# Gate tanh tiles in a ring of their own, alternating parities in the Toeplitz products, later copies of the powers, and two merge gates loaded early, in a hybrid S5 and dilated-attention layer

## The chip, the cores and the metric

The kernel runs on one core of a Trainium2 chip. The metric is the device time of one execution in microseconds (us). A core has a matmul engine (PE, with a separate weight-load row PEld in the profile), a vector engine (DVE), a scalar engine (ACT), a general engine (POOL), and a queue engine (SP) that here only issues transfers. All run their own instruction streams in order and wait for each other through semaphores. Matmul results land in PSUM, which has eight banks; everything else lives in SBUF, in 128 partitions.

## The reference, cut to what matters

One decoder layer of 512 tokens with 1024 channels, in float32. One projection feeds two branches and two merge gates:

```python
h = rms_norm(x, norm_w)
u_s, z_s, q, k, v, z_a, r_s, r_a = split(h @ w_in)
y_s = s5_branch(u_s, ...)                  # diagonal complex scan, GELU, GLU with w_glu
y_s = (y_s * silu(z_s)) @ w_ssm_out
y_a = dilated_attention(norm_rope(q), norm_rope(k), v)   # 3 dilations, 8 heads of 64
y_a = (y_a * silu(z_a)) @ w_attn_out
m = sigmoid(r_s) * y_s + sigmoid(r_a) * y_a
out = x + m @ w_o
```

The sigmoid is computed as a tanh of half the argument: sigmoid(r) = (tanh(r/2) + 1)/2, and silu likewise; the halves are folded into later scales.

## The kernel before, in words

**Matmuls.** A float32 product is made from three fp32r matmuls (`mm3`, L108 to L110): each operand is split into a high part (ACT, L93) and a remainder (DVE, L95), and high x high, high x low and low x high are added up in PSUM. A projection unit (`cm_unit`) takes 128 output channels for all 512 tokens: 8 blocks of the contraction by 3, so 24 matmuls of 128x512 into one bank named `pj`. In the first half of the program there are three such banks and five general ones (tag `g`); in the second half four, three and one for attention outputs. Weights arrive by SP (`w_raw`, two buffers of 512 KB), are split by ACT and DVE into `w_hi` and `w_lo` (three buffers each), and are fetched two units ahead.

**Stages.** (1) Norm of x and its transposes; the input u of the S5 branch, eight units. (2) Powers of the 64-state transition: they are computed on DVE with groups along partitions (`pw`), turned by small matmuls against an identity into `atp` (32 matmuls in one bank: i is the real or imaginary part, k the power) and `ftp` (4 matmuls, a factor for B), and copied by ACT into `AT` (L405) and `fT` (L411). `AT` feeds all coefficient products (`coef`, L261 to L263) and the scan; `fT` feeds `BB`. (3) The S5 branch in chunks of 8 time steps: `w_unit` and `x_unit` make the chunk inputs, DVE scans over chunks (`scan_work`), and for each of eight blocks j: `ca_unit` makes coefficients, `m_unit` the Toeplitz block (products `kps`, 16 matmuls of 64x16 weights against 128 columns on tiles of the array given by `tile_position`; ACT copies to `kt`, POOL adds the skip term and sends eight transfers into M), `y_unit` the outputs (`yps`) and `g_unit` the transposes (`yT`) and the GELU (`gs`, `gq`). Between them stand "fillers": gate units of the same projection, in the order za (4), zs (8), two for v, rs (8), ra (2). (4) GLU with w_glu, then w_ssm_out with the gate r_s, giving `m1`. (5) Attention for four pairs of heads, with projections of q, k and v between scores and values; the remaining six ra units lie here, one ahead of the pairs and five behind the last scores. (6) w_attn_out in eight blocks c: the gate is loaded (`ral`, L1103), DVE forms (ral + 1) x projection + m1 (L1108, L1109), which is split for the last product with w_o; the residual x is loaded whole (`xr`, 2 MB) and added.

**Gates.** Every gate unit ends in one tanh on ACT from its `pj` bank into a tile `th`. For za and zs (`silu2`) DVE multiplies at once. For rs and ra the tile is stored in DRAM (`gd[1, c]`, `rad[c]`) by SP and loaded again when it is used.

**Buffers and order.** The helper `t2k` hands out tiles of 128x512 from a ring of six buffers with one tag. `th`, `ysb`, `gs`, `gq`, `z`, `ral` and others share it. A tile's buffer becomes free when the last reader is through, a transfer included. The framework orders the instructions: each engine gets a fixed list, drawn up when the program is built from a simulated timeline, the order of the text serving as priority. So the lists can differ from the text, and an edit in one place can change them elsewhere. It also sets all waits; instructions that touch one PSUM bank wait for each other.

Of the kernel before, what the change touches and what calls it, by code (L numbers as in the profile page):

```python
# [11 lines left out]
F32 = mybir.dt.float32  # L12
# [8 lines left out]
P = 128  # L21
# [6 lines left out]
Q = 16  # L28
# [24 lines left out]
def tile_hybrid_block(ctx: ExitStack, tc: tile.TileContext, x, positions, norm_w, w_in, lam_re, lam_im,  # L53
# [3 lines left out]
    pe, act, dve, pool, sp = nc.tensor, nc.scalar, nc.vector, nc.gpsimd, nc.sync  # L57
# [5 lines left out]
    tmp = ctx.enter_context(tc.tile_pool(name="tmp", bufs=6))  # L63
# [21 lines left out]
    def bank(name):  # L85
        return ps_g.tile([P, 512], F32, name=name, tag="g")

    def t2k(name, dtype=F32):
        return tmp.tile([P, 512], dtype, name=name, tag="t2k")
# [23 lines left out]
    n_ra = 2  # L113
# [66 lines left out]
    def cm_unit(rh, rl, kts=KT):  # L180
        hi, lo = get_w()
        ps = ps_p.tile([P, 512], F32, name="pj", tag="pj")
        for k in range(kts):
            mm3(ps, hi[:, k], lo[:, k], rh[:, k], rl[:, k], k == 0, k == kts - 1)
        return ps
# [28 lines left out]
    for h in range(2):  # L214
# [10 lines left out]
        for q in range(KT // 2):  # L225
            ps = bank("hps")
# [133 lines left out]
    pw = big.tile([G, 2, 9, N], F32, name="pw", tag="s7a")  # L360
# [20 lines left out]
    for n in (1, 2, 4):  # L381
# [3 lines left out]
        a = pw[:, :, 0:n, :]  # L385
# [6 lines left out]
    H = G // 2  # L392
    AT = cst.tile([P, 2, H, 9], F32, name="AT")
    fT = cst.tile([P, 2, H], F32, name="fT")
    pool.memset(AT[:, 0, :, 8:9], 1.0)
    pool.memset(AT[:, 1, :, 8:9], 0.0)
    idg = ident[:G, :G].rearrange("p (m two) -> p two m", two=2)
    ps = bank("atp")
    for i in range(2):
        for k in range(8):  # L400
            for h in range(2):
                o = i * 8 * H + (7 - k) * H
                pe.matmul(ps[64 * h:64 * h + 64, o:o + H], pw[:, i, k], idg[:, h], start=True, stop=True,
                          skip_group_check=True)
        act.copy(AT[:, i, :, 0:8], ps[:, i * 8 * H:(i + 1) * 8 * H].rearrange("p (k g) -> p g k", k=8))  # L405
    ps = bank("ftp")
    for i in range(2):
        for h in range(2):
            pe.matmul(ps[64 * h:64 * h + 64, i * H:(i + 1) * H], pw[:, i, 8], idg[:, h], start=True, stop=True,
                      skip_group_check=True)  # L410
    act.copy(fT.rearrange("p a g -> p (a g)"), ps[:, 0:2 * H])  # L411

    A4 = cst.tile([P, 2, 2, H], F32, name="A4")
    for i in range(2):
# [7 lines left out]
    BB = dd[:, 2560:4096].rearrange("p (a g q) -> p a g q", a=3, g=H)  # L422
# [29 lines left out]
    sza = cst.tile([P, NP, S], F32, name="sza")  # L452
    gd = dram.tile([2, KT, P, S], F32, name="gd")

    def silu2(dst, ps):

        th = t2k("th")
        act.activation(th, ps, AF.Tanh, scale=0.5)
        dve.scalar_tensor_tensor(dst, th, 1.0, ps, op0=ALU.add, op1=ALU.mult)

    def za_unit(c):
        ps = cm_unit(hT_hi, hT_lo)
        silu2(sza[:, c], ps)
# [6 lines left out]

    def rs_unit(c):
        ps = cm_unit(hT_hi, hT_lo)
        th = t2k("th")
        act.activation(th, ps, AF.Tanh, scale=0.5)  # L474
        sp.dma_start(gd[1, c], th)

    rad = dram.tile([KT, P, S], F32, name="rad")

    def ra_unit(c):
        ps = cm_unit(hT_hi, hT_lo)  # L480
        th = t2k("th")
        act.activation(th, ps, AF.Tanh, scale=0.5)  # L482
        sp.dma_start(rad[c], th)

# [43 lines left out]
    for g in range(NG):  # L528
        for a in range(2):
# [3 lines left out]
                      start=True, stop=True, skip_group_check=True)  # L533
# [31 lines left out]
    def v0_unit(hp, V):  # L565
        ps = cm_unit(hT_hi, hT_lo)
        vt = t2k("vt")
        act.copy(vt.rearrange("p (b r j) -> p r b j", r=4, b=4), ps.rearrange("p (r b j) -> p r b j", r=4, b=4))

        def finish():  # L570
            pt = bank("vtp")
            for b in range(NB):
                pe.transpose(pt[:, b * P:(b + 1) * P], vt[:, b * P:(b + 1) * P], ident)
            act.copy(V[:, 0].rearrange("p b c -> p (b c)"), pt)
        return finish
# [17 lines left out]
    H = G // 2  # L593
# [105 lines left out]
    def m_unit(j, ca, dg):  # L699

        kt = big.tile([Q, 8, T, Q], F32, name="kt", tag=("s7a", "s7b")[j % 2])
        ps = bank("kps")
        for gg in range(8):
            a, b, h, m = gg % 4, gg // 4, gg % 2, gg // 2
            for c in range(2):
                sl = slice(64 * h, 64 * h + 64)
                pe.matmul(ps[32 * a:32 * a + Q, b * P:(b + 1) * P], BB[sl, 1 + c, 4 * j + m, :], ca[sl, c, m, 1:9, :],  # L707
                          start=c == 0, stop=c == 1, skip_group_check=True, tile_position=(64 * h, 32 * a))
        kv = kt.rearrange("q (b a) k p -> q a b (k p)", a=4)
        for a in range(4):  # L710
            act.copy(kv[:, a], ps[32 * a:32 * a + Q, 0:2 * P].rearrange("q (b m) -> q b m", b=2))  # L711
        pool.tensor_tensor(kt[:, :, T - 1, :], kt[:, :, T - 1, :], dg, op=ALU.add)  # L712

        M = Mb[j % 3]
        for t in range(T):
            pool.dma_start(M[Q * t:Q * t + Q, :, 0:P - Q * t], kt[:, :, t:].rearrange("q g k p -> q g (k p)"))  # L716
        return M
# [118 lines left out]
    def qk_turn(g, raw, QT, KA, KB):  # L836
        for a in range(2):
            ps = bank("qtp")
            pn = ps.rearrange("p (b r j) -> p r b j", r=4, b=4)
            for r in range(NB):  # L840
                o = pn[:, r] if g == 0 else ps[:, r * P:(r + 1) * P]
                pe.transpose(o, raw[:, r, a * P:(a + 1) * P], ident)  # L842
            if a == 0 or g == 0:
                parts = [(slice(0, P), QT[0][:, g], QT[1][:, g]) if a == 0 else (slice(0, P), KA[0], KA[1])]
            else:
                parts = [(slice(64 * h, 64 * h + 64), KB[0][64 * h:64 * h + 64, g - 1, h],
                          KB[1][64 * h:64 * h + 64, g - 1, h]) for h in range(2)]
            for sl, hi, lo in parts:
                w = wcol[sl, g, a:a + 1]
                act.activation(hi, ps[sl], AF.Copy, scale=w)  # L850
                dve.scalar_tensor_tensor(lo, ps[sl], w, hi.bitcast(F32), op0=ALU.mult, op1=ALU.subtract)  # L851
# [9 lines left out]
    def qk_first(mid=None):  # L861

        pss = wide_granule(hT_hi, hT_lo, mid)
        raws = [new_raw(0), new_raw(1)]
        sq = sml.tile([P, NB, 8], F32, name="ssq")
        for r in range(NB):
            for i in range(2):
                act.copy(raws[i][:, r], pss[r][:, 256 * i:256 * i + 256])
            squares(sq[:, r], pss[r])
        qk_norm((0, 1), raws, sq)  # L870
        return raws

    def qk_second(hp, mid=None):

        pss = wide_granule(hT_hi, hT_lo, mid)
        raw = new_raw(0)
        V = new_v()
        sq = sml.tile([P, NB, 8], F32, name="ssq")[:, :, 0:4]
        for r in range(NB):
            act.copy(raw[:, r], pss[r][:, 0:256])  # L880
            squares(sq[:, r], pss[r][:, 0:256])
            act.copy(V[:, 1:3, r], pss[r][:, 256:512].rearrange("p (g c) -> p g c", g=2))
        qk_norm((2,), [raw], sq)
        return raw, V
# [138 lines left out]
    for c in range(KT):  # L1023
# [5 lines left out]
        ps = cm_unit(gT_hi, gT_lo)  # L1029
        th = t2k("gth")  # L1030
# [4 lines left out]
    for c in range(KT):  # L1035
        r = t2k("rl")
        sp.dma_start(r, gd[1, c])
        ps = cm_unit(yT_hi, yT_lo)
# [28 lines left out]
    ra_unit(n_ra)  # L1067
    qk_turn(2, raw, *QK)

    for hp in range(NP):  # L1070
        Pt = scores(hp, *QK)
        if hp < NP - 1:
            raws = qk_first()

            def mid(kq):
                if kq in (1, 2):
                    qk_turn(kq - 1, raws[kq - 1], *QK)
                if kq == 3:
                    values(hp, Pt, V)

            raw, V_next = qk_second(hp + 1, mid)
            V = V_next
            finv = v0_unit(hp + 1, V)
            qk_turn(2, raw, *QK)
            finv()
        else:
            for c in range(n_ra + 1, KT - 2):
                ra_unit(c)
            values(hp, Pt, V)
            for c in range(KT - 2, KT):  # L1090
                ra_unit(c)
# [6 lines left out]
    for cc in range(KT // 2):  # L1098
        hi, lo = get_w()
        for c2 in range(2):  # L1100
            c = 2 * cc + c2
            th = t2k("ral")
            sp.dma_start(th, rad[c])  # L1103
            ps = ps_p.tile([P, 512], F32, name="pj", tag="pj")
            for k in range(NP):
                mm3(ps, hi[:, k, c2 * P:(c2 + 1) * P], lo[:, k, c2 * P:(c2 + 1) * P], aT[:, 0, k], aT[:, 1, k],
                    k == 0, k == NP - 1)
            dve.scalar_tensor_tensor(th, th, 1.0, ps, op0=ALU.add, op1=ALU.mult)  # L1108
            dve.tensor_tensor(th, th, m1[:, c], op=ALU.add)  # L1109
            split(mT_hi[:, c], mT_lo[:, c], th, scale=0.5)  # L1110
# [38 lines left out]
```

## Time and profile before

| | us |
|---|---|
| median of 3 runs | 743.11 (741.96 to 743.18) |
| profiled execution, its time | 742.37 |
| profiled execution, its span | 740.6 |
| PE busy | 699.8 (94%) |
| DVE busy | 454.2 (61%) |
| ACT busy | 314.8 (43%) |
| POOL busy | 193.9 (26%) |
| mean granted clock of PE | 0.987 |

In the profile's rows, "idle 5.6 <-ACT th L474" or "[1.59 <-ACT th L474]" is idle time of an engine and the instruction that ended it. Timeline rows give the start, the duration, the engine, the line of the kernel, the operation and the tiles as out<-in; "x4" means that several instructions are merged into one row. SPq rows are the issue of transfers, not their landing. A float32 matmul outside `mm3` is recorded as two instructions, so 16 matmuls of a Toeplitz unit are 32 in the profile. In windows, "(x8)" behind an engine's busy time is the number of its instructions, and the three last figures are the granted clock of PE, the share of the transfer engines and GB/s.

### The profile page before, as it was taken

Reading aid. Unit: us, or ns where it says so; the run is one execution under the profiler, and the core shown is the slowest. Engines: PE = TensorE matmul, PEld = TensorE weight load, DVE = VectorE, ACT = ScalarE, POOL = GpSimd, SP = SyncE. Lnnn points to the kernel's source line nnn. Section 1 sums busy time; section 2 is a strip of 40 time slices with the busy share of each in tenths; the row PEclk is TensorE's granted clock in tenths of the full one; section 3 lists DMA queues with packets and bytes.
Section 4 is the critical chain, followed back from the end, with each engine's and each line's share of the span. In section 5 each row is a group of like instructions: output and inputs, shape, how many; then the busy total and the mean of one; then the engine's idle time right before and its main releaser. Section 6 shows DMA issues by size and latency. Waiting matters only on the chain.

```text
span 740.6 us, 12691 instructions
## 1 busy us (share of the span) xinstructions
PE 699.8 (94%) x4821; PEld 572.7 (77%) x4821; DVE 454.2 (61%) x912; ACT 314.8 (43%) x631; POOL 193.9 (26%) x346
## 2 busy tenths in 40 slices
PE   2789999999999898999999999999999989998997
PEld 2778878789877686888889888787778767887886
DVE  6859746989755743673426669647663765464742
ACT  6434543423244564431244465437344643543310
POOL 3426720421122522540002316012412232120000
PEclk9999999999999999999999999999999999999999
DMA  8334654554454644555332322222302230327441
GB/s 203 102 100 129 170 115 104 141 144 120 117 118 106 119 117 129 171 171 170 86 96 80 101 82 85 58 85 58 96 20 86 58 115 12 106 97 240 131 142 57
DMA packets 137213, 82.14 MB, mean 111 GB/s; under 512 B 32696, under 2 KB 125632, under 8 KB 137024
## 3 DMA queue, kind: packets, MB, share of 16 engines
q1 hardware_dynamic: 135088, 78.96, 37.5%
q0 software_dynamic: 2048, 2.36, 2.3%
q8 instruction: 38, 0.62, 0.4%
q14 instruction: 23, 0.19, 0.1%
q10 hardware_dynamic: 16, 0.00, 0.0%
HBM read 68.46 MB, written 10.49 MB: 107 GB/s over the span
## 4 chain that ended last, share of the span: by engine, by line
PE 88%; ACT 4%; DMA 3%; SPq 2%; DVE 2%; issue 0%; ACTq 0%; DVEq 0%
PE pj L108 24%; PE pj L110 24%; PE pj L109 24%; PE ptp L999 2%; DMA w_raw<-in_w_in_dram 2%; PE ot L985 2%; PE kps L707 1%; DMA ral<-rad 1%; PE yps L731 1%; PE yps L738 1%; PE xps L293 1%; PE wps L282 1%; PE sps L929 1%; ACT w_hi L93 1%; PE qtp L842 1%; SPq L426 1%
## 5 line engine op out<-in xcount | busy, mean ns | idle before, releaser
L93 ACT ACTIVATE w_hi<-w_raw 128x1024 fp32r<-128x1024 f32 x100 | 106.0, 1061 | 233.2 <-PE pj L109 133.7
L95 DVE TENSOR_TENSOR w_lo<-w_raw,w_hi 128x1024 fp32r<-128x1024 f32 x98 | 123.7, 1262 | 120.1 <-ACT w_hi L93 119.5
L108 PE MATMUL pj<-hT_hi,w_hi 128*128 128x512 f32 (+1 forms) x344 | 133.1, 390 | 7.8 <-ACT th L474 5.6
L109 PE MATMUL pj<-hT_lo,w_hi 128*128 128x512 f32 (+1 forms) x344 | 132.5, 386 | 4.1 <-DVE hT_lo L236 4.1
L110 PE MATMUL pj<-hT_hi,w_lo 128*128 128x512 f32 (+1 forms) x344 | 132.4, 386 | 0.8 <-DVE w_lo L95 0.8
L109 PE MATMUL pj<-w_lo,hT_hi 128*128 128x512 f32 (+1 forms) x288 | 106.5, 370 | 0.0
L108 PE MATMUL pj<-w_hi,hT_hi 128*128 128x512 f32 (+1 forms) x288 | 106.5, 371 | 0.0
L110 PE MATMUL pj<-w_hi,hT_lo 128*128 128x512 f32 (+1 forms) x288 | 106.0, 371 | 0.0
L108 PEld LDWEIGHTS pj<-hT_hi,w_hi 128*128 128x128 f32 x344 | 65.0, 190 | 22.8 <-ACT th L474 6.8
L109 PEld LDWEIGHTS pj<-hT_lo,w_hi 128*128 128x128 f32 x344 | 65.4, 190 | 17.5 <-DVE hT_lo L236 4.9
L110 PEld LDWEIGHTS pj<-hT_hi,w_lo 128*128 128x128 f32 x344 | 65.5, 190 | 14.4 <-DVE w_lo L95 1.0
L108 PEld LDWEIGHTS pj<-w_hi,hT_hi 128*128 128x128 f32 x288 | 54.0, 188 | 10.1 <-issue 0.2
L110 PEld LDWEIGHTS pj<-w_hi,hT_lo 128*128 128x128 f32 x288 | 54.0, 188 | 10.0
L109 PEld LDWEIGHTS pj<-w_lo,hT_hi 128*128 128x128 f32 x288 | 54.0, 188 | 9.8
L908 ACT ACTIVATE Pt<-Pt,st 128x256 f32<-128x256 f32 (+1 forms) x64 | 31.0, 491 | 18.7 <-DVE st L906 18.7
L829 POOL TENSOR_TENSOR rt<-qraw,tC 128x256 f32<-128x256 f32 x12 | 14.3, 1190 | 87.7 <-DVE qraw L823 87.4
L712 POOL TENSOR_TENSOR kt<-kt,dg 16x128 f32<-16x128 f32 x8 | 5.6, 702 | 116.8 <-ACT kt L711 116.8
L716 POOL DMA_DIRECT2D dd<-kt x64 | 33.8, 537 | 2.4 <-POOL kt L712 2.4
L938 POOL COPY sw<-st 32x4 f32<-32x4 f32 x64 | 12.0, 188 | 73.1 <-ACT Pt L908 70.4
L851 DVE SCALAR_TENSOR_TENSOR qkp<-qtp,wcol,qkp 128x512 fp32r<-128x512 f32 (+1 forms) x32 | 23.0, 745 | 13.2 <-ACT qkp L850 13.1
L850 ACT ACTIVATE qkp<-qtp,wcol 128x512 fp32r<-128x512 f32 (+1 forms) x32 | 20.8, 686 | 15.7 <-PE qtp L842 10.4
L108 PE MATMUL pj<-gT_hi,w_hi 128*128 128x512 f32 x64 | 24.9, 391 | 2.6 <-ACT th L482 2.6
(267 smaller groups left out, 1306.5 us busy)
## 6 DMA issues: line engine op xcount, KB each, us to landing
w_raw<-in_w_in_dram SPq DMA_DIRECT2D x40, 512.0 KB
w_raw<-in_w_in_dram SPq DMA_DIRECT2D x112, 128.0 KB
w_raw<-in_w_glu_dram SPq DMA_DIRECT2D x8, 512.0 KB
w_raw<-in_w_ssm_out_dram SPq DMA_DIRECT2D x8, 512.0 KB
w_raw<-in_w_o_dram SPq DMA_DIRECT2D x8, 512.0 KB
x_all<-in_x_dram SPq DMA_DIRECT2D x4, 512.0 KB
ud<-uT SPq DMA_DIRECT2D x8, 256.0 KB
Uj<-ud SPq DMA_DIRECT2D x8, 256.0 KB
```

The source lines that it names most:

```text
L93: act.activation(hi, src, AF.Copy, scale=scale)
L95: e.tensor_tensor(lo, src, hi.bitcast(F32), op=ALU.subtract)
L108: pe.matmul(o, lh, rh, start=first, stop=False, skip_group_check=True)
L109: pe.matmul(o, lh, rl, start=False, stop=False, skip_group_check=True)
L110: pe.matmul(o, ll, rh, start=False, stop=last, skip_group_check=True)
L716: pool.dma_start(M[Q * t:Q * t + Q, :, 0:P - Q * t], kt[:, :, t:].rearrange("q g k p -> q g (k p)"))
L829: pool.tensor_tensor(t1, rh[:, :, :, 0:16], cv.broadcast_to([P, NB * 2, 2, 16]), op=ALU.mult)
L850: act.activation(hi, ps[sl], AF.Copy, scale=w)
L851: dve.scalar_tensor_tensor(lo, ps[sl], w, hi.bitcast(F32), op0=ALU.mult, op1=ALU.subtract)
L908: act.activation(o, o, AF.Exp, bias=nm, scale=-1.0, accum_out=st[:, kind, 1, h, b:b + 1])
L985: pe.matmul(o, v, pts[h][:, (2 * i + k) * P:(2 * i + k + 1) * P], start=first, stop=kind == 1 and b == NB - 1 and k == 1, skip_group_check ...
L999: pe.transpose(ps[:, (2 * i + k) * P:(2 * i + k + 1) * P], Pt[:, h, kind, 2 * bb + i, k * P:(k + 1) * P], ident)
```

## The change

Four edits.

1. The tanh tiles get a ring of their own with two buffers (`gate_tile`): in `silu2`, in all rs units and in the ra units up to number 2. The later ra units keep the common ring.
2. In `m_unit` the 16 matmuls are issued in another order: before, both matmuls of one output (c) followed each other and the partition half h changed with every second one; now h changes with every one, and the outputs are done in two groups of two array tiles (a0 = 0, 2).
3. The copies of `AT` stand behind all matmuls of `atp` and `ftp` and behind the copy of `fT`; before, the first copy stood between the matmuls of the real and the imaginary half.
4. The merge gates of blocks 0 and 1 are loaded into the gate ring ahead of the last ra units; the others are loaded where they were.

```diff
@@ powers
-        act.copy(AT[:, i, :, 0:8], ps[:, i * 8 * H:(i + 1) * 8 * H].rearrange("p (k g) -> p g k", k=8))
-    ps = bank("ftp")
+    pf = bank("ftp")
     for i in range(2):
         for h in range(2):
-            pe.matmul(ps[64 * h:64 * h + 64, i * H:(i + 1) * H], pw[:, i, 8], idg[:, h], start=True, stop=True,
+            pe.matmul(pf[64 * h:64 * h + 64, i * H:(i + 1) * H], pw[:, i, 8], idg[:, h], start=True, stop=True,
                       skip_group_check=True)
-    act.copy(fT.rearrange("p a g -> p (a g)"), ps[:, 0:2 * H])
+    act.copy(fT.rearrange("p a g -> p (a g)"), pf[:, 0:2 * H])
+    for i in range(2):
+        act.copy(AT[:, i, :, 0:8], ps[:, i * 8 * H:(i + 1) * 8 * H].rearrange("p (k g) -> p g k", k=8))
@@ gates
+    def gate_tile():
+        return tmp.tile([P, 512], F32, name="th", tag="th", bufs=2)
...
-        th = t2k("th")                                  # silu2 and rs_unit
+        th = gate_tile()
...
-        th = t2k("th")                                  # ra_unit
+        th = gate_tile() if c <= n_ra else t2k("th")
@@ m_unit
-        for gg in range(8):
-            a, b, h, m = gg % 4, gg // 4, gg % 2, gg // 2
-            for c in range(2):
-                sl = slice(64 * h, 64 * h + 64)
-                pe.matmul(ps[32 * a:32 * a + Q, b * P:(b + 1) * P], BB[sl, 1 + c, 4 * j + m, :], ca[sl, c, m, 1:9, :],
-                          start=c == 0, stop=c == 1, skip_group_check=True, tile_position=(64 * h, 32 * a))
+        for a0 in (0, 2):
+            for b in range(2):
+                for c in range(2):
+                    for h in range(2):
+                        a, m = a0 + h, 2 * b + a0 // 2
+                        sl = slice(64 * h, 64 * h + 64)
+                        pe.matmul(ps[32 * a:32 * a + Q, b * P:(b + 1) * P], BB[sl, 1 + c, 4 * j + m, :],
+                                  ca[sl, c, m, 1:9, :], start=c == 0, stop=c == 1, skip_group_check=True,
+                                  tile_position=(64 * h, 32 * a))
@@ attention, behind the last scores, ahead of the last ra units
+            for c in range(2):
+                rals[c] = gate_tile()
+                sp.dma_start(rals[c], rad[c])
@@ merge
-            th = t2k("ral")
-            sp.dma_start(th, rad[c])
+            if c in rals:
+                th = rals[c]
+            else:
+                th = t2k("ral")
+                sp.dma_start(th, rad[c])
```

More of the change, by code (lines that the diff above doesn't have):

```diff
@@ L472, in rs_unit @@
         ps = cm_unit(hT_hi, hT_lo)
-        th = t2k("th")
+        th = gate_tile()
         act.activation(th, ps, AF.Tanh, scale=0.5)
@@ L480, in ra_unit @@
         ps = cm_unit(hT_hi, hT_lo)
-        th = t2k("th")
+        th = gate_tile() if c <= n_ra else t2k("th")
         act.activation(th, ps, AF.Tanh, scale=0.5)
@@ L1068, in tile_hybrid_block @@
     qk_turn(2, raw, *QK)
+    rals = {}
     for hp in range(NP):
```

## The prediction

> **What bounds the kernel.** I read the page first (busy time of the engines, the chain that ended last), then the list of waits of the matmul engine (PE), then the clock by windows. The waits' figures are us in total, times, and the longest.
>
> ```profile
> PE 699.8 (94%) x4821; PEld 572.7 (77%) x4821; DVE 454.2 (61%) x912; ACT 314.8 (43%) x631; POOL 193.9 (26%) x346
> PE 88%; ACT 4%; DMA 3%; SPq 2%; DVE 2%; issue 0%; ACTq 0%; DVEq 0%
> ...
> PE pj L108 <- ACT th L474: 5.6, 3, 2.2
> PE qtp L842 <- DVE qkp L851: 3.5, 2, 1.8
> PE atp L403 <- ACT AT L405: 2.4, 1, 2.4
> PE pj L108 <- ACT th L482: 2.6, 1, 2.6
> PE pj L108 <- DVE ral L1108: 2.2, 1, 2.2
> ```
>
> PE is busy 94% and is 88% of the chain, so time is won only by taking away its waits or its work. Three waits belong to the edited code: gates (L474, L482) 5.6 + 2.6 = 8.2 us, powers 2.4, the first merge gate 2.2. A wait can cost more than its length:
>
> ```profile
> 244.10:247.50 3.40, 3.37 (x8) 2.69 (x9) 3.37 (x5) 0.63 (x1) 2.06 (x4) 0.50 0.69 135
> 286.80:290.20 3.40, 3.40 (x16) 2.82 (x15) 2.22 (x2) 0.81 (x2) 1.96 (x2) 1.00 0.92 256
> 681.00:684.40 3.40, 3.40 (x10) 2.66 (x9) 3.40 (x5) 1.26 (x2) 0.00 (x0) 0.50 0.67 191
> 684.40:687.80 3.40, 3.40 (x17) 2.80 (x16) 3.40 (x7) 0.31 (x1) 0.00 (x0) 1.00 0.86 266
> ```
>
> Each row is a stretch; the first count is matmuls, the third figure from the end the granted clock. Behind the gate wait at 244.1 and the merge-gate wait at 680.4 the clock is 0.50 for 3.4 us: 8 matmuls run where 16 do at full clock, and 10 where 17 do. At 3.4/16 and 3.4/17 us each that is 1.7 and 1.4 us more. Behind the wait of 2.6 us (286.0) the clock is 1.00, so not every wait brings it. The Trainium skill, "TensorE: Matmul & The Clock Gate", Part 1, says the clock halves after an idle window of about 3.4 us. By that rule waits of 2.2 us would not halve it; the rows show that they do, and the measurement decides.
>
> **Powers copied behind all matmuls.**
>
> ```profile
> 46.62 0.66 PE L403 MATMUL atp<-ident,pw 64*64 64x32 f32 x16
> 54.14 1.06 ACT L93 ACTIVATE w_hi<-w_raw 128x1024 fp32r<-128x1024 f32 x1 [5.52 <-DMA w_raw<-in_w_in_dram]
> 55.10 0.35 ACT L405 COPY AT<-atp 128x256 f32<-128x256 f32 x1
> 55.51 1.24 PE L403 MATMUL atp<-ident,pw 64*64 64x32 f32 x32 [2.44 <-ACT AT L405]
> 60.28 0.40 PE L110 MATMUL pj<-hT_hi,w_lo 128*128 128x512 f32 x1
> 60.51 0.40 PE L108 MATMUL pj<-hT_hi,w_hi 128*128 128x512 f32 x1
> 55.23 1.23 DVE L95 TENSOR_TENSOR w_lo<-w_raw,w_hi 128x1024 fp32r<-128x1024 f32 x1 [6.67 <-ACT w_hi L93]
> ...
> 60.60:204.00 143.40, 143.40 (x1060) 117.05 (x1059) 115.95 (x162) 55.35 (x110) 45.44 (x53) 1.00 0.50 131
> ```
>
> The last row is a window. The first half's matmuls end at 47.3. Its copy (AT, L405) stands on ACT behind a split that waits for weights until 54.14, and the second half, in the same bank, waits for the copy. After the change no matmul waits for a copy: the second half runs with the first, where PE is busy, so its 1.2 us only move. Gone are 2.44 us of idling and the slow clock behind it: at 0.50 a matmul takes 3.4/8 = 0.43 us, at full clock 0.23 (60.28 to 60.51), and some 7 of this unit's fall into the slow stretch: 7 x 0.2 = 1.4. Sum 3.8. What is late next: the unit would end at 60.5 - 3.8 = 56.7, and the next one's split weights are ready at 55.23 + 1.23 = 56.46, so no new wait. The copy of fT now stands behind more matmuls; its products feed the same coefficients as AT, which they get at 55.45 today, so some 8 us cover it, and beyond that each us is one for the coefficients. The two AT copies may stay behind the split as now: nothing is worse then. From 60.6 to 204 PE is busy for all 143.4 us, so what is won is carried on. Ends: 0 (PE waits for weights instead) and 3.8; I take 3.8, from the rows of the place itself.
>
> **Gates in buffers of their own.**
>
> ```profile
> 217.78 0.63 ACT L755 ACTIVATE gq<-gs 128x512 f32<-128x512 f32 x1
> 218.31 0.58 ACT L474 ACTIVATE th<-pj 128x512 f32<-128x512 f32 x1
> 218.94 0.50 PE L108 MATMUL pj<-hT_hi,w_hi 128*128 128x512 f32 x1 [1.59 <-ACT th L474]
> 284.35 0.62 ACT L755 ACTIVATE gq<-gs 128x512 f32<-128x512 f32 x1
> 284.87 1.07 ACT L482 ACTIVATE th<-pj 128x512 f32<-128x512 f32 x2
> L474 ACT ACTIVATE th<-pj x8: 578/580/605, 206.0 to 279.0; 128x512 f32<-128x512 f32 x8
> ```
>
> Both tanhs shown follow at once on the first gq of a g_unit, and at 284.87 two run back to back, though their projections are a unit of 24 matmuls (24 x 0.23 = 5.6 us) apart: the first had long been ready. I read from this that the six buffers of the common ring are handed out in the order of the text: a tanh written behind gs and gq gets none until those have theirs. Meanwhile its projection holds one of three PSUM banks, and PE waits for a bank (218.94). With a ring of its own the tanh runs when its projection ends. The rounds contract by what PE waited, unless the chain of y_units holds them:
>
> ```profile
> 222.36 0.76 DVE L263 TENSOR_TENSOR ab<-ab 128x576 f32<-128x576 f32 x1
> 224.74 0.39 PE L707 MATMUL kps<-ab,dd 64*16 64x128 f32 x2
> 288.71 1.22 DVE L97 SCALAR_TENSOR_TENSOR gT_lo<-gq,gT_hi 128x512 fp32r<-128x512 f32 x1 [0.70 <-ACT gT_hi L93]
> ```
>
> The coefficients for kps are ready at 223.1, and PE comes at 224.74: 1.6 us of slack, just that round's wait. So I give the three waits in full, 5.6, and the slow stretch 1.7. Of the last 2.6 less: the GLU would start at 283.4, reach its last three matmuls 21 x 0.23 = 4.8 later at 288.2, and wait for gT_lo, done at 289.9; of 2.6 only 0.9 is won. Sum 5.6 + 1.7 + 0.9 = 8.2; ends 0 (rival 2) and 8.2 + 1.7 = 9.9. The 4 za and 8 zs gates also change buffers; no wait of theirs is on PE: 0. The gates' stores are none added, only issued earlier on SP. The common ring loses a user and can only hand out sooner.
>
> **Parities alternate.**
>
> ```profile
> 129.80 0.39 PE L707 MATMUL kps<-ab,dd 64*16 64x128 f32 x2
> 178.44 1.09 PE L707 MATMUL kps<-ab,dd 64*16 64x128 f32 x32
> L707 PE MATMUL kps<-ab,dd x256: 269/269/280, 129.8 to 262.2; 64*16 64x128 f32 x128
> L707 PEld LDWEIGHTS kps<-ab,dd x256: 88/93/93, 129.8 to 262.1; 64*16 64x16 f32 x128
> ```
>
> Same work in another order. A merged row lasts from its first start to its last end, so two instructions of one tile start 0.39 - 0.27 = 0.12 us apart; 32 together start every (1.09 - 0.27)/31 = 0.027 us. So the four tiles of the array that a unit uses already run at once. The old order puts the fourth tile's first instruction 13th and it still overlaps; the new one puts the second pair 17th, so at most 4 places are missing, at two per step two steps of 0.12: 0.2 us a unit, 1.9 for eight. Ends: 1.9 lost, 0.7 a unit won (below). I take 0, for at four tiles at once there is nothing left to fill.
>
> **Two merge gates early.**
>
> ```profile
> 669.27 0.34 SPq L1112 DMA_DIRECT2D xr<-in_x_dram  x1
> 669.66 1.61 SPq L1103 DMA_DIRECT2D ral<-rad  x2
> 679.61 1.36 DVE L1108 SCALAR_TENSOR_TENSOR ral<-ral,pj 128x512 f32<-128x512 f32 x2 [7.73 <-DMA ral<-rad]
> ```
>
> The first load is issued behind the 2 MB of xr and lands 9.9 us later. DVE would be free for it from 671.9 (679.61 - 7.73). Loaded early, gate 0 is multiplied when its projection ends, and PE finds a bank where it now starts to wait, at about 678.2 (the wait of 2.2 ends behind the product of 0.7 that starts at 679.61): 2.2 and the slow stretch's 1.4 go, 3.6. Gate 2 is late next: if it lands with the same 9.9 us at about 679.6, its bank is wanted two units of 12 matmuls later, near 678.2 + 5.5 = 683.7. The two loads move on SP, 0.33 us each, anywhere behind the store of ra unit 2; a weight load queued behind would find two loaded units (11 us) as cover. DVE's own row of products starts 2.5 us earlier too. Ends 0 (gate 2 takes the place) and 3.6; I take 3.6.
>
> **Sum.** 3.8 + 8.2 + 0 + 3.6 = 15.6. The order on all engines is planned anew, and a plan draws waits of its own: I charge one of 1.8 us (the longest qtp wait above) with a slow stretch of 1.5, 3.3 in all, so 12.3 are left. The profiled execution took 742.37, 1.8 more than its span, giving 730.1; the median of the three runs is 743.11, 0.7 higher, so I say 730.8.
>
> **Rivals.**
> 1. The tail lies bare (0.12): PE spends the gate units early, and the last y_unit has no cover.
>
> ```profile
> 264.95 4.18 POOL L716 DMA_DIRECT2D dd<-kt  x8 [0.30 <-POOL kt L712]
> 266.90 0.66 PE L748 MATMUL yT<-ident,ysb 128*128 128x128 f32 x4
> 282.90 0.34 SPq L1025 DMA_DIRECT2D zl<-gd  x1
> 285.80 1.67 POOL L1028 TENSOR_TENSOR zl<-zl,gsum 128x512 f32<-128x512 f32 x1 [1.86 <-DMA zl<-gd]
> SPq L174 <- DVE w_lo L95: 23.4, 8, 6.3
> ```
>
> Its M is issued by 269.1 and lands some 2.9 us later (the zl load, 282.90 to 285.80), so at 272; PE without gate units is through at 267.3: 4.7 idle and 1.5 of slow clock, 6.2 in all: 737.0. Against: before, PE had gate units left there.
> 2. The tanhs stay late (0.08), because something other than the ring holds them: only 3.8 + 3.6 - 3.3 = 4.1, so 739.0. For it: the ring is inferred. Against: the strict place behind gq.
> 3. The half clock stays (0.06): its stretches have another cause; without 1.4 + 1.7 + 1.4 it is 735.3. The rule of the Trainium skill above amounts to this case.
> 4. kps falls to two tiles at once (0.05): 16 steps for 8, 0.9 us a unit, 7 in all: 737.8. Against: the 13 places shown.
> 5. The alternation uncovers weight loads (0.03): eight loads a unit by 0.09 us, 0.7 a unit, 5.8: 725.0. The Trainium skill, "TensorE: Matmul & The Clock Gate", "The mechanism" (Part 3), says a weight load overlaps running matmuls only where the row group differs; the four-fold overlap above leaves it nothing.
> 6. Slower (0.06): two gate buffers are too few. A buffer is free once its store has landed. SP stands up to 6.3 us for weight buffers with stores queued behind, and a transfer lands after up to 9.9 us (ral, beside xr). Such a store takes 16.2 us and exceeds two units (11.2) by 5, spent on ACT, with the weight splits and the kt copies behind. It decides once the ten stored gates before the GLU (8 rs, 2 ra) lose the 12.3 us: 1.2 each, a store of 12.4. At 2 each the time is 750.8, which I give it; at 5 each it would be 781. Against: the eight rs gates come (279.0 - 206.0)/7 = 10.4 us apart, so two are 21.
> The remaining 0.02 is waits that cancel the gain.
>
> **Numbers.** The forecast has 0.58, with 724 to 736 as its own range (no new wait, or two). For 8 in 10 I reach from 724 (no new wait and the upper ends) to 740 (rivals 1 to 4). A measurement of this kernel can tell about 0.2%, 1.5 us, from no change. Faster 0.90: forecast and rivals 1 to 5, nearly whole; same 0.04; slower 0.06.
>
> **What would show it.** Right: the rows of PE waiting for AT, th and ral are gone; L474 directly follows its projection; the half clock at 56, 244 and 681 is gone; a kps unit of 32 still spans 1.1 us. Wrong: a wait of ACT for a gate's store, a longer kps unit, PE waiting for yps or gT near the start of the GLU, new waits over 2 us elsewhere.

## The result, and the profile after

The changed kernel takes 735.63 us (median of 4 runs, 734.15 to 736.66) against 743.14 us before (4 runs, 741.96 to 743.52): the ratio is 0.9892, interval 0.9864 to 0.9920. That is 7.5 us won, where the prediction had 12.3. The profiled execution took 736.25 us with a span of 734.5 us.

The page after; PE's busy time has not changed (699.8 us before), so what is gone is waiting, but less of it than forecast:

```profile
PE 700.5 (95%) x4821; PEld 574.7 (78%) x4821; DVE 456.8 (62%) x912; ACT 314.5 (43%) x631; POOL 191.8 (26%) x346
PE 86%; DMA 4%; ACT 3%; DVE 3%; SPq 3%; issue 1%; ACTq 0%
```

PE's list of waits after (us in total, times, longest):

```profile
PE hps L231 <- DVE x_all L224: 9.4, 1, 9.4
PE xps L293 <- DMA Uj<-ud: 3.9, 2, 3.5
...
PE qtp L850 <- DVE qkp L859: 3.5, 2, 1.8
...
PE pj L110 <- DVE w_lo L95: 1.6, 2, 0.9
...
PE pj L108 <- ACT gs L761: 1.0, 1, 1.0
...
PE wps L282 <- DVE ab L263: 0.4, 1, 0.4
```

The rows for AT, th and ral are gone, as forecast. The wait for hps at the start, 9.4 us, is as long as before. New are Uj (3.9 us), which comes next, a second wait for w_lo, and small ones for gs and ab. The chain says the same: DMA has 4% of it, and before 3%.

Windows of the changed kernel, with the clock as the third figure from the end. The first is a new slow stretch; the two at 244 and 681 were at 0.50 before:

```profile
34.60:41.40 6.80, 5.92 (x28) 5.88 (x28) 6.61 (x28) 0.91 (x2) 0.36 (x1) 0.50 0.00 0
244.10:247.50 3.40, 3.40 (x107) 3.10 (x106) 0.56 (x1) 2.72 (x9) 1.42 (x3) 1.00 0.57 154
681.00:684.40 3.40, 3.40 (x17) 2.81 (x16) 3.40 (x7) 1.19 (x2) 0.00 (x0) 1.00 0.82 293
```

To see where the time went I cut every trace at the starts of the same matmuls: the first powers matmul (`atp`), the last `xps`, the first GLU product, the first product of w_attn_out, and the first of w_o. Each figure of the table is a difference of two such times in one profiled execution. The last stretch (w_o to the end) is 47.6 us in all of them.

| kernel | to atp | atp to xps end | to GLU | to w_attn_out | to w_o | atp to GLU |
|---|---|---|---|---|---|---|
| before | 42.3 | 77.2 | 166.5 | 373.5 | 33.4 | 243.7 |
| after | 45.5 | 76.9 | 162.1 | 373.1 | 29.3 | 239.0 |
| gates_only | 44.2 | 76.2 | 160.2 | 373.0 | 31.0 | 236.4 |
| merge_only | 43.3 | 77.7 | 164.9 | 374.9 | 29.3 | 242.6 |
| powers_only | 44.2 | 80.1 | 168.0 | 373.6 | 30.8 | 248.1 |
| gates_merge | 45.0 | 76.8 | 159.8 | 372.8 | 29.3 | 236.6 |
| no_parity | 44.1 | 78.1 | 159.8 | 373.0 | 29.3 | 237.9 |
| no_powers | 43.0 | 75.4 | 162.1 | 374.4 | 29.3 | 237.5 |
| after_held | 45.3 | 78.8 | 162.4 | 372.9 | 29.3 | 241.2 |
| best | 42.8 | 79.4 | 159.8 | 372.9 | 29.3 | 239.2 |
| kps_four | 45.5 | 78.0 | 158.2 | 374.4 | 29.3 | 236.2 |
| kps_bytile | 42.9 | 77.2 | 168.8 | 371.5 | 29.3 | 246.1 |
| split_first | 42.6 | 73.7 | 160.1 | 373.1 | 29.3 | 233.8 |
| split_four | 45.5 | 73.3 | 158.1 | 372.8 | 29.3 | 231.4 |

The second and third columns do not hold the same work in every kernel. With edit 1, PE's list has 12 projection matmuls fewer ahead of the last xps and 12 more behind it, some 2.8 us at 0.23 us each, against 3 small matmuls (cps) the other way: the traces have 614 matmul instructions between these two marks where before has 623. So these columns compare only among before, merge_only and powers_only, or among the others. Across, the last column does, their sum, with 2328 instructions in every kernel.

Before to after: 3.1 us lost ahead of the powers; 4.7 won from there to the GLU, where 3.8 and 8.2 were forecast; 0.5 in the next stretch; 4.1 before w_o. Together, before rounding, 6.1, the difference of the two profiled executions (742.37 and 736.25).

### The profile page after: what moved, and what is told of

It reads as the page before. It is cut to its first block, busy times and chain, and to the rows that moved or that the text cites. A ratio compares the mean times of both kernels' runs of the same rounds, so it can differ in the third digit from the quotient of the medians.

```text
span 734.5 us, 12680 instructions
## 1 busy us (share of the span) xinstructions
PE 700.5 (95%) x4821; PEld 574.7 (78%) x4821; DVE 456.8 (62%) x912; ACT 314.5 (43%) x631; POOL 191.8 (26%) x346
## 4 chain that ended last, share of the span: by engine, by line
PE 86%; DMA 4%; ACT 3%; DVE 3%; SPq 3%; issue 1%; ACTq 0%
PE pj L108 24%; PE pj L110 23%; PE pj L109 23%; DMA w_raw<-in_w_in_dram 3%; PE ot L993 2%; PE ptp L1007 2%; PE kps L714 2%; PE yps L739 1%; PE yps L746 1%; DMA Uj<-ud 1%; PE xps L293 1%; PE sps L937 1%; PE qtp L850 1%; SPq L427 1%; ACT w_hi L93 1%
## 5 line engine op out<-in xcount | busy, mean ns | idle before, releaser
L93 ACT ACTIVATE w_hi<-w_raw 128x1024 fp32r<-128x1024 f32 x100 | 106.0, 1061 | 239.0 <-PE pj L109 132.4
L859 DVE SCALAR_TENSOR_TENSOR qkp<-qtp,wcol,qkp 128x512 fp32r<-128x512 f32 (+1 forms) x32 | 23.0, 745 | 13.3 <-ACT qkp L858 13.2
L858 ACT ACTIVATE qkp<-qtp,wcol 128x512 fp32r<-128x512 f32 (+1 forms) x32 | 20.8, 685 | 15.7 <-PE qtp L850 10.4
L262 POOL TENSOR_TENSOR ab<-dd,AT 128x512 f32<-128x512 f32 x16 | 23.0, 1447 | 10.8 <-DVE ab L263 10.8
```

The lines of the kernel that those rows point to most:

```text
L93: act.activation(hi, src, AF.Copy, scale=scale)
L262: eng.tensor_tensor(tv, a2.unsqueeze(2).broadcast_to(sh), ai, op=ALU.mult)
```

## The second stretch: how the powers' gain was lost

Three PE rows of the changed kernel's timeline, then DVE's rows of the same place:

```profile
65.41 1.26 PE L282 MATMUL wps<-ident,ab 128*128 128x128 f32 x8 [0.38 <-DVE ab L263]
68.01 0.50 PE L110 MATMUL pj<-hT_hi,w_lo 128*128 128x512 f32 x1 [0.87 <-DVE w_lo L95]
84.29 1.15 PE L293 MATMUL xps<-Uj,W 128*64 128x64 f32 x32 [3.48 <-DMA Uj<-ud]
```

```profile
59.43 2.68 DVE L261 TENSOR_TENSOR ab<-dd,AT 128x512 f32<-128x512 f32 x4
62.03 1.05 DVE L606 TENSOR_TENSOR scn<-A 128x32 f32<-128x32 f32 x1
...
64.68 1.28 DVE L263 TENSOR_TENSOR ab<-ab 128x512 f32<-128x512 f32 x2
65.88 2.08 DVE L95 TENSOR_TENSOR w_lo<-w_raw,w_hi 128x1024 fp32r<-128x1024 f32 x1
```

The same place before, on DVE, and then on SP:

```profile
58.92 0.22 DVE L602 TENSOR_TENSOR scn<-A 128x32 f32<-128x32 f32 x1
59.07 1.21 DVE L95 TENSOR_TENSOR w_lo<-w_raw,w_hi 128x1024 fp32r<-128x1024 f32 x1
60.21 1.05 DVE L603 TENSOR_TENSOR scn<-A 128x32 f32<-128x32 f32 x1
```

```profile
60.31 0.37 SPq L174 DMA_DIRECT2D w_raw<-in_w_in_dram  x1
```

SP after:

```profile
60.88 0.59 SPq L271 DMA_DIRECT2D ud<-uT  x1
67.98 0.37 SPq L174 DMA_DIRECT2D w_raw<-in_w_in_dram  x1
...
77.10 0.63 SPq L250 DMA_DIRECT2D Uj<-ud  x1
```

Before, the first powers matmul started at 42.34 and the first wps at 66.11; after, these are 45.45 and 65.41. So by 65 us the powers had won their 3.8 us ((66.11 - 42.34) - (65.41 - 45.45)). But with AT complete 2.4 us earlier (its last copy ends 15.7 us behind the first powers matmul before, 13.3 after), small scan-table products (`scn`) and the coefficient adds (L263) are ready early too, and in DVE's list they now stand ahead of the third split. `w_lo` ends at 67.96 and not at 60.28. The next weight load needs the buffer that this split frees, so SP stands from 61.5 to 67.98. In the window row of this gap hardly anything is moved (25 GB/s):

```profile
60.00:64.00 4.00, 4.00 (x19) 3.23 (x18) 4.00 (x7) 1.43 (x2) 4.00 (x5) 1.00 0.64 172
64.00:68.00 4.00, 2.77 (x15) 1.61 (x13) 4.00 (x6) 1.47 (x2) 2.67 (x3) 1.00 0.07 25
```

All later weights come late, and Uj behind them in SP's queue: PE loses 0.87 and 3.48 us. That was a reading; the experiments test it.

## The experiments

The first four leave one part out or keep one alone. Theory A was: the powers edit hands its gain back through the scan tables' place on DVE, and the alternating order costs 1.9 us. Theory B: the powers are worth their 3.8 us, and the loss has another cause. Theory C: the longer Toeplitz unit is covered by other work.

**gates_merge: edits 1 and 4 alone** (AT's copies and the order of the Toeplitz products as before: the two diffs that follow, together).

> Only the gate ring and the two early merge gates; the powers and the Toeplitz products as before. Theory A (the powers edit wins its wait and hands it back, since it lets DVE put the scan tables ahead of a weight split, and the parity order costs 1.9 us): about 8 from the gates and 4 from the merge gates, 743.1 - 12 = 731; PE waits for AT once (2.4 us) with a half clock behind it, no wait for Uj. Theory B (the powers edit is worth its 3.8 us, and what is lost early in the changed kernel has another cause): 735.6 + 3.8 - 1.9 = 737.5.

Measured 731.94 us (0.9856, 0.9804 to 0.9909), less than the full change (0.9892), with intervals that overlap. The Uj wait is not in its list; the AT wait is back with 2.5 us. So nothing here shows that edits 2 and 3 together help.

**no_parity: the change without edit 2.** Against the changed kernel:

```diff
-        for a0 in (0, 2):
-            for b in range(2):
-                for c in range(2):
-                    for h in range(2):
+        for gg in range(8):
+            a, b, h, m = gg % 4, gg // 4, gg % 2, gg // 2
+            for c in range(2):
...
```

> The changed kernel with the old order of the Toeplitz products. Theory A (kps falls to two tiles at once for part of each unit): a unit of 32 spans 1.09 us again instead of 1.51, the eight units give back 1.9 us, 733.7. Theory C (the longer unit is covered, since the chain of y_units and not PE sets that stage): the same 735.6, with 2 us of new PE waits there.

Measured 732.92 (0.9883, 0.9852 to 0.9914). In the table the stretch to the GLU is 159.8 us and not 162.1, so by the traces the longer unit is not covered, and theory C falls. The Uj wait stays with 3.5 us.

**no_powers: the change without edit 3.** Against the changed kernel:

```diff
+        act.copy(AT[:, i, :, 0:8], ps[:, i * 8 * H:(i + 1) * 8 * H].rearrange("p (k g) -> p g k", k=8))
...
-    for i in range(2):
-        act.copy(AT[:, i, :, 0:8], ps[:, i * 8 * H:(i + 1) * 8 * H].rearrange("p (k g) -> p g k", k=8))
```

> The changed kernel with the powers copied as before. Theory A: 731 + 1.9 = 733, better than the changed kernel by 2 to 3 us: the wait for AT is back, the waits for w_lo and Uj at 68 and 84 are gone. Theory B: worse by 3.8, 739.4.

Measured 731.88 (0.9872, 0.9847 to 0.9898). No Uj wait; the stretch to the GLU is 162.1 us. Twice, then, with and without the powers edit, the alternating order costs 162.1 - 159.8 = 2.3 us there; a third pair, after_held and best below, has 2.6. The timed intervals of these kernels overlap, so the traces carry this and the times only agree in sign.

**powers_only: edit 3 alone.** Against the kernel before it is the last diff turned round, with `pf` for the second bank.

> Only the powers edit. Theory A: 743 within 1.5 us, AT wait gone, new waits of PE for w_lo and Uj between 60 and 95 us of some 4.5 us. Theory B: 739.3, no wait for Uj.

Measured 745.43 (1.0047, 1.0020 to 1.0074): alone it makes the kernel slower, by about 0.5%. PE's waits have no row for AT, but

```profile
PE xps L293 <- DMA Uj<-ud: 3.8, 1, 3.8
```

The stretch from atp to the end of xps is 80.1 us, 2.9 more than before, for the same work. Theory B falls: it gave 739.3.

**after_held: the change, with the scan tables queued late on DVE.** `coefs` collects the adds of `coef`; `issue_after` only orders instructions of one engine.

```diff
+    coefs = []
...
-        dve.tensor_tensor(dst, dst, tv, op=ALU.add)
+        coefs.append(dve.tensor_tensor(dst, dst, tv, op=ALU.add))
...
+    def held_tables():
+        with tc.issue_after(coefs[11].ins):
+            scan_tables()
-    scan_work = [scan_tables]
+    scan_work = [held_tables]
```

> The changed kernel with all four edits; added is only an order: the scan tables' VectorE instructions (17 small ones and one copy of 128x1024) are queued behind the twelfth coefficient product of the S5 stage, so that they no longer stand ahead of the third weight split. Theory A (the powers edit hands its gain back because these tables go ahead of a weight split on VectorE): the waits xps<-Uj of 3.5 us near 84 us and w_lo of 0.9 us near 68 us are gone, the start of kps lies about 4.5 us earlier than in the changed kernel measured from the first wide product, and the whole is 4 to 5 us under the changed kernel, 0.983 of the kernel before (about 728.7). Theory B (the late load Uj has a cause of its own, the copies' new order on ScalarE or the SP queue): the wait at 84 us stays, 0.989 of before (about 733.3). Rival: the tables, now at 75 to 100 us, hold up something else (a scan step or the gates' products), and the gain comes back elsewhere.

Measured 735.37 (0.9897, 0.9868 to 0.9927): no gain. Theory A in this narrow form was wrong. Uj still costs 4.5 us.

**best: the same without edit 2.**

> The gates', powers' and merge gates' edits with the scan tables queued late as in after_held, and the Toeplitz products in their old order. Theory A, with 1.9 us for the longer unit of the parity order: 1.9 us under after_held, 0.980 to 0.981 of before (about 727). If the longer unit is covered by other work (theory C): the same as after_held within 0.5 us.

Measured 733.97 (0.9874, 0.9833 to 0.9915). Its DVE rows say why the tables alone did not help:

```profile
60.51 2.14 DVE L265 TENSOR_TENSOR ab<-ab 128x512 f32<-128x512 f32 x2 [0.95 <-POOL ab L264]
62.57 2.08 DVE L95 TENSOR_TENSOR w_lo<-w_raw,w_hi 128x1024 fp32r<-128x1024 f32 x1
```

The tables are no longer there, and now two adds that wait for POOL's product stand ahead of the split. Its atp started 2.6 us earlier than in the changed kernel (42.82 and 45.45), so a split at 62.57 is late again, against 59.07 before with atp at 42.34.

**split_first: best, and the adds of the first two W units behind the splits they overtook.** `los` collects the splits.

```diff
+        k = {0: 6, 1: 6, 2: 7, 3: 7}.get(len(coefs))
+        with tc.issue_after(los[k].ins) if k else ExitStack():
-        coefs.append(dve.tensor_tensor(dst, dst, tv, op=ALU.add))
+            coefs.append(dve.tensor_tensor(dst, dst, tv, op=ALU.add))
```

> best (gates', powers' and merge gates' edits, tables late) with one more order on VectorE: the adds of the first two W units' coefficient products stand behind the weight splits w_lo that they overtook, as in the kernel before. Theory A in its wider form (with the powers early, whatever is ready first on VectorE, tables or coefficient adds that wait for GpSimd, goes ahead of the split that frees the weight buffer; the loads pause 4 to 5 us and Uj comes late behind them): w_lo starts near 59.5 us and not at 62.57, the next weight load near 61 and not at 64.68, the slices without DMA traffic around 63 us are gone, the Uj wait of 4.3 us is under 1 us, first wide product to end of xps takes 75 us or less (best 79.4, before 77.2), and the whole is about 4 us under best, 0.982 of before. Theory F (the stage is bound by its weight and Uj loads whatever VectorE's order, so the 3.8 us of the powers could never be carried on): the Uj wait or another one of 3 to 4 us stays before 100 us, and the time is best's, 0.987.

Measured 728.59 (0.9799, 0.9771 to 0.9826), 5.4 us under best, with intervals that do not touch. Its DVE and its waits:

```profile
59.28 2.08 DVE L97 TENSOR_TENSOR w_lo<-w_raw,w_hi 128x1024 fp32r<-128x1024 f32 x1
61.29 2.15 DVE L269 TENSOR_TENSOR ab<-ab 128x512 f32<-128x512 f32 x2
```

```profile
61.39 0.37 SPq L176 DMA_DIRECT2D w_raw<-in_w_in_dram  x1
```

```profile
PE xps L299 <- DMA Uj<-ud: 1.4, 2, 0.8
PE pj L112 <- DVE w_lo L97: 0.8, 1, 0.8
```

The split starts at 59.28, the weight load behind it is issued at 61.39 (64.68 in best), and Uj's wait falls from 4.3 to 1.4 us (I had expected under 1). The stretch from atp to the end of xps takes 73.7 us, 5.7 under best; of this, up to 3.4 is a half clock of 6.8 us that follows the Uj wait in best and is missing here. Against the kernels with edit 1 but without edit 3 (76.2, 76.8 and 75.4 in gates_only, gates_merge and no_powers) it is 1.7 to 3.1, where the prediction had 3.8. So the place of these splits on DVE is shown to be what took the powers' gain away: theory F, which held the stage bound by its loads whatever the order, falls.

Next, two orders of the same 16 Toeplitz products, on top of best.

**kps_four: all four array tiles in turn, matmul by matmul.**

```diff
+        for b in range(2):
+            for c in range(2):
+                for a in range(4):
+                    h, m = a % 2, 2 * b + a // 2
...
```

> best with another order of the Toeplitz products: all four array tiles in turn, matmul by matmul (loops b, c, a), so that consecutive matmuls alternate in row half as in the parity edit, but over four tiles and not two. Theory D (an array tile takes its instructions in order, about four of them can wait or run at a tile, and the instruction stream stops behind a full one): all four tiles run from the first step, 8 steps of about 0.13 us, a unit spans 1.0 to 1.1 us as in the old order, time as best within 1 us. Theory E (alternation of the row halves itself costs, by a weight load that can't be hidden or the like): a unit of 32 instructions spans 1.4 to 1.6 us as in the changed kernel, and the time is about 2 us over best.

Measured 732.80 (0.9859, 0.9812 to 0.9906), 1.2 us under best, with intervals that overlap.

**kps_bytile: the same with the loops a, b, c**, so that a tile's eight instructions stand in a row.

> best with the Toeplitz products of one array tile all in a row (loops a, b, c: eight instructions of one tile, then the next tile). Theory D (about four instructions deep at a tile, issue in order): the tiles overlap only by half, 20 steps of 0.11 us, a unit spans about 2.2 us, in groups of 1,1,1,1,2,2,2,2 and so on, and the eight units cost 6 to 9 us more than in best. Theory E (alternation costs, runs in one tile are cheap): a unit spans 1.1 us or less, and the time is that of best. A queue as deep as eight or more: 8 steps, 1.1 us, the time of best.

Measured 742.70 (0.9999, 0.9974 to 1.0024), 8.7 over best. One unit of 32 instructions lasts, in the changed kernel, in kps_four and in kps_bytile:

```profile
184.41 1.51 PE L714 MATMUL kps<-ab,dd 64*16 64x128 f32 x32
```

```profile
184.71 1.06 PE L718 MATMUL kps<-ab,dd 64*16 64x128 f32 x32
```

```profile
184.01 2.40 PE L718 MATMUL kps<-ab,dd 64*16 64x128 f32 x32
```

Before it was 1.09, as it is in best. From these less the last instruction's 0.27, in steps of 0.11 to 0.12: 8 steps before and in kps_four (the last group starts at step 7), 12 after, 20 in kps_bytile. Theory D gave 8 and 20 ahead of these runs; the changed kernel's trace, with its 12, was there when the theory was made. In kps_bytile the single starts come in groups of 1 (four times), then 2 (twelve times), then 1 (four times), 32 in 20 steps; after, 2 (four times), 4 (four times), 2 (four times). The trace has the starts but not the tiles, so what follows is theory D's reading of them: a tile takes its instructions one after the other, a following tile gets its first one when the tile ahead has some four left, and a run of eight on a tile keeps the next tile empty for a while, which a run of four does not (five to seven were not run). Alternation in itself costs nothing (theory E falls): over four tiles it is as short as the old order. The Trainium skill, "TensorE: Matmul & The Clock Gate", "The mechanism" (Part 3), says matmuls start and end strictly in program order. For kps_bytile a tile's first start would then come with the eighth of the tile ahead at the earliest, at least 29 steps in all; the row's 20 are against it. This takes PE's list to have the text's order, which the units that start early bear out: they pause behind 2 instructions in best and kps_bytile, 4 in the changed kernel and 8 in kps_four, where the text has the first product with the second coefficient half.

PE's busy time for the 256 instructions in the window from 120 to 285 us, after and in kps_four:

```profile
120.00:285.00 165.00, 13.31 (x256) 8.63 (x256) 1.00 0.52 130
```

```profile
120.00:285.00 165.00, 9.84 (x256) 5.62 (x256) 1.00 0.53 135
```

In best, with the order of before, it is 11.4:

```profile
120.00:285.00 165.00, 11.37 (x256) 7.06 (x256) 1.00 0.52 131
```

That kps_four is lower than this does not come from the 32-unit, which is as long. It fits that kps_four starts 8 and not 2 instructions of a unit before the second coefficient half is ready; no run tests this apart.

**split_four: split_first with the four-tile order.**

> split_first with the four-tile order of the Toeplitz products. By the queue theory PE is busy 9.8 us there and not 11.4, and what of it counts is at most 1.5 us: 0 to 1.5 us under split_first. The fastest of all if theory A's wider form holds, 0.980 to 0.982 of before.

Measured 726.74 (0.9774, 0.9753 to 0.9796), the fastest here. To the GLU it needs 158.1 us and split_first 160.1, as kps_four and best (158.2 and 159.8); the timed intervals overlap.

**gates_only: edit 1 alone**, against the kernel before (the first `th` in `silu2` and `rs_unit`, the second in `ra_unit`):

```diff
+    def gate_tile():
+        return tmp.tile([P, 512], F32, name="th", tag="th", bufs=2)
...
-        th = t2k("th")
+        th = gate_tile()
...
-        th = t2k("th")
+        th = gate_tile() if c <= n_ra else t2k("th")
```

> The gates' edit alone. The prediction's term: the four waits for th (5.6 us in the profile before) are gone, with the half clock behind them and part of the last one; the stretch from the first y product to the GLU is 73 to 75 us and not 81.5, the wait before the merge (ral) stays at 1 to 2.3 us with its half clock, and the time is 0.989 to 0.990 of before (735). If the gates were worth only their plain waits: 0.9925.

Measured 731.22 (0.9839, 0.9809 to 0.9868), 12.0 us, more than expected. In the profiled execution 7.2 us are won from atp to the GLU, 0.6 behind it and 2.4 before w_o; the waits for th are gone, and one I had not given to this edit is shorter (2.2 us before):

```profile
PE pj L108 <- DVE ral L1111: 1.3, 1, 1.3
```

That last part is not shown to be the edit's: powers_only, which touches neither gates nor merge gates, has 1.2 us for this wait, no half clock behind it, and 30.8 us in the stretch before w_o. The profiled execution, 734.05 us, is the slowest of the four timed ones, so the 12.0 has some clock luck in it (below).

**merge_only: edit 4 alone**, against the kernel before, with a `gate_tile` that nothing else uses:

```diff
+            for c in range(2):
+                rals[c] = gate_tile()
+                sp.dma_start(rals[c], rad[c])
...
```

> The merge gates' edit alone (two buffers of their own, loaded before the last values). The prediction's term: the wait for ral before the merge (2.2 us in the kernel before) and the half clock behind it (1.4) are gone, the stretch from the first output projection of attention to the first w_o product is 29.3 to 30 us and not 33.4, 3.6 us in all, 0.995 of before. With the gates' edit alone that stretch had already fallen to 31.0, so that the two edits share this gain: together they gave 4.1 there, and if the shares overlap the merge alone takes 3 to 4; if they only add up, 1.6 (0.998).

Measured 741.80 (0.9995, 0.9974 to 1.0017): no difference that can be told, against 3 to 4 us expected; the other value on record, 1.6 us (0.998), lies inside the interval. In its profiled execution (739.51 us) the stretch before w_o is 29.3 us and not 33.4, and no ral wait is left. But powers_only and gates_only, without this edit, have 30.8 and 31.0 there, with a ral wait of 1.2 and 1.3 us and no half clock. So against these two the edit wins 1.5 to 1.7 us there and not 4.1; the rest is a longer wait and a half clock that before has and not every kernel without the edit. The ten timed runs differ by their granted clock: at 0.987 and 0.988 they took 739.0 to 739.6 us (four runs), at 0.981 743.5 to 744.5 (four runs); all but one of the runs of before beside them lie at 0.986 to 0.988. What lowers the clock in some executions of this kernel, and where, was not traced and stays open.

## Why the prediction was right and wrong

The direction and the range held; the sum of 15.6 less 3.3 was too high by 4.8. Two of the prediction's own signs of being wrong came true, a longer kps unit and a new wait over 2 us.

- **Powers, 3.8.** Won, as shown by the start of wps: the wait of 2.44 and the 1.4 for the slow clock behind it (the row below, from the kernel before) make up the 3.8 found there. It was handed back within 20 us, and more with it: alone, the edit costs 2.9 us up to the end of xps. The step that failed is "From 60.6 to 204 PE is busy for all 143.4 us, so what is won is carried on". A PE that is always busy in the old trace says nothing of how close its inputs follow. The question "what is late next" was asked only of the next unit's w_lo (56.46) and not of the split after it, which stood on DVE among products that the edit makes ready sooner. What turned the gain into a loss was the edit's effect on DVE's list, not on PE's. With the order repaired the term is 1.7 to 3.1, by the kernel it is held against.

```profile
56.30:59.80 3.50, 3.50 (x19) 2.79 (x16) 3.50 (x7) 1.75 (x3) 2.58 (x5) 0.51 0.58 160
```

- **Charge of 3.3 for one new wait.** A guess without a place. A new wait came, 3.48 in one piece, with 0.87 in another, so the charge was near it in size, and by that luck the sum was not further off.
- **Gates, 8.2.** In traces 7.2 alone from atp to the GLU, where the term lies. The mechanism was right: no wait for th is left, the tanhs come earlier (the row below; 206.0 to 279.0 before), and the slow clock at 244 is gone. Of the last wait of 2.6, for which 1.7 were left to a late gT_lo, the changed kernel has 1.0 at the GLU's start, but for gs; no wait for gT_lo is in its list.

```profile
L478 ACT ACTIVATE th<-pj x8: 574/578/583, 201.5 to 262.1; 128x512 f32<-128x512 f32 x8
```

- **Parity, 0.** This term was mis-sized: a loss of 2.3, 2.3 and 2.6 us in three pairs of traces. Its own lower end was 1.9. The step was "for at four tiles at once there is nothing left to fill": the order can leave tiles empty that were full. The forecast row "a kps unit of 32 still spans 1.1 us" came out as 1.51. Rival 4 had the direction, at three times the size (16 steps for the 12 found); rival 5 fell, for a unit of 32 is no shorter with alternation (1.06 and 1.09 us).
- **Merge gates, 3.6.** 4.1 of the stretch before w_o in the trace, but 1.5 to 1.7 against powers_only and gates_only, in which the wait was already shorter and the half clock gone. How long this wait is and whether the half clock follows it varies between kernels that have the same code there, and the prediction took one profile's values for the edit's. Both edits together have 11.9 from atp to the end of the span (686.3 us in gates_merge, 698.2 before), where 8.2 + 3.6 = 11.8 was said; that it comes out so near is in part luck, by the above. By itself the edit could not be told from nothing in timed runs.
- **Half clock (rival 3).** The stretches at 244 and 681 went with their waits. But 6.8 us of half clock at 34.6 appeared, ahead of everything the change touches, and cost most of the 3.1 us of the first stretch. It lies at 34 to 35 in after, gates_merge, after_held, kps_four and split_four, is shorter or elsewhere in the others (split_first, whose program is that of split_four up to there, has 3.4 us at 26.3), and is missing in before alone. Up to the first powers matmul PE, ACT and SP run the same instructions in the same order in before and after. I take it for chance, neither a cost of the change nor a credit. Leaving the first stretch out, before to after is 9.2 us and not 6.1.
- **Bare tail and late tanhs (rivals 1 and 2).** PE waits 1.0 us ahead of the GLU, not 4.7, and gates_only, which changes the ring alone, has no wait for th, so it was the ring that held the tanhs.
- **Slower (rival 6).** No ACT wait for a gate's store was seen.

## What to carry over

Ask of an edit that makes data ready earlier what else becomes ready with it on every in-order engine, and whether that overtakes an instruction that frees a buffer of the load queue; look at that engine's list, not at the busy share of the one that should gain. Price an order of small matmuls on array tiles by runs per tile: four instructions in a row kept the neighbours busy here, eight did not. Before comparing stretches between markers, count the instructions in them, for an edit can move work across a marker. Where a stall can halve the clock, compare stretches between markers and not only totals.

## What the runs showed of the hardware

The half clock comes in pieces of 3.4 us, single or double (the last one is cut by the end of the trace), and the length of a wait does not decide it. The Uj wait of 3.48 us in the changed kernel brings none (84 to 88 us run at 1.00), that of no_parity, as long, brings 3.4 us, and that of best, 4.3, brings 6.8, while the wait of 1.8 us for qkp was followed by it at 536:

```profile
536.40:539.80 3.40, 3.40 (x19) 2.42 (x18) 2.04 (x4) 1.27 (x2) 0.00 (x0) 0.50 0.10 29
```

The Trainium skill, "TensorE: Matmul & The Clock Gate", Part 1, tells of a free-running window of 3.4 us; pieces of 3.4 us and the dependence on chance agree with that, while the rule that a whole idle window is needed does not agree with the wait of 1.8: from 533.0 to 536.4, the piece ahead of the row, PE was busy for 1.75 us. One kernel's time moves by it: gates_merge ran from 725.11 us at a mean clock of 0.997 to 733.95 at 0.985.
